# One-hot tiles of the expert gates, laid out by token

## The chip, the cores and the metric

The kernel runs on one core of a Trainium2 chip. A core has five engines that run side by side, each through a queue of its own: TensorE (PE in the profile; its weight loads are the separate row PEld), VectorE (DVE), ScalarE (ACT), GpSimd (POOL) and SyncE (SP, which here only issues DMAs). The metric is the device time of one launch in microseconds, lower being better; the number to predict is the median of the kernel after the change, against the median of the kernel before.

## The reference

Eight stages run on 256 tokens of width 1024: a retention layer, a PEER expert layer, differential attention, a second PEER layer, a gated feed-forward layer, a mixer, and a last feed-forward layer, with normalisations between them. The change touches the two PEER layers alone. Cut to what matters, one of them is:

```python
q = (xc @ w_q).reshape(tokens, 8, 2, 128)
sc = einsum('thpd,hpnd->thpn', q, subkeys)         # 8 heads, 2 halves, 128 keys each
s1, i1 = top_k(sc[:, :, 0], 16)
s2, i2 = top_k(sc[:, :, 1], 16)
top, pos = top_k(s1[..., :, None] + s2[..., None, :], 16)   # over the 256 pairs
idx = take(i1 * 128 + i2, pos)                     # 8 * 16 = 128 experts of 16384 per token
gate = softmax(top)
act = gelu(einsum('ted,td->te', u[idx], xc))
y = einsum('te,ted->td', gate * act, v[idx])
```

## The kernel before, in words

`peer` doesn't gather rows of `u` and `v`. It computes the activation of all 16384 experts for all 256 tokens and multiplies it with a gate that is zero for every expert not chosen. The activations stand in the tile `H` of 128 partitions (first key) x 128 (second key, `i2`) x 256 tokens.

A loop over the 128 values of `i2` fills `H`. Each turn takes one 512 KB block of `u` from the SP queue (`stream`, L136), splits it on ACT into a rounded half `wh` (L125) and on DVE into the rest `wl` (L126), and runs 24 matmuls of 256 columns on PE (`gemm_a`, L147 to L149). ACT then writes the gelu (L1245, or L1248 and L1250), and for the tokens whose gates are done already, DVE multiplies them in (L1251). The tiles `wh` and `wl` have three buffers each.

The router's top-k work runs on DVE beside the first turns (`route_keys`, `route`). At its end `qd` holds, by token, 128 slots with four numbers each: the first key, the second key, and the high and low part of the gate, scaled by 2^15. PE transposes the four 128 x 128 blocks of each half of the tokens (L1422) and ACT copies them into the tile `slotT`: 128 partitions (slots) x 4 numbers x 256 tokens, two bytes each (L1423).

From turn `K0` = 44 on, the 64 batches of four tokens of a layer are handled, spread over the turns up to 126. For one batch

- `onehots` has DVE compare the two index rows with the key numbers `iota4` into `o12` (L1437; the profile calls this tile `o`), and multiply the second half with the two gate parts into `og` (L1438). Both tiles come from the pool `peer_oh` with two buffers, and both have the tokens innermost: 2 x 128 keys x 4 tokens. `iota4` holds each key number four times for that.
- `gates` has PE multiply, for each token, the one-hot of the first key (weights, 128 x 128) with the two gated one-hots of the second key (256 moving columns) into `gat`, a PSUM tile with two buffers (L1448). Both operands are read with a step of four elements. ACT copies the low part out of PSUM (L1452).
- a turn later, `apply` has DVE add the high part (L1455) and multiply the gates into the finished part of `H` (L1456), and ACT copy the rest (L1458).

So a layer has 64 batches, the kernel 128, and PE runs 512 of the L1448 matmuls. The order of the instructions on each engine is set ahead of the run by a scheduler that goes by the order of the code, the raised priority of `stream` and its own estimates of times; each engine then runs its queue in order. A buffer is written again only when the last reader of its former content is done. After the loop come the 128 turns of the second product (L1276), which the change doesn't touch.

Of the kernel before, what the change touches and what calls it, by code (L numbers as in the profile page):

```python
# [12 lines left out]
F16 = mybir.dt.float16  # L13
BF16 = mybir.dt.bfloat16
U32 = mybir.dt.uint32
AF = mybir.ActivationFunctionType
ALU = mybir.AluOpType
# [3 lines left out]
T = 256  # L21
# [46 lines left out]
class Ker:  # L68
# [1096 lines left out]
    def peer(s, l, xs, units_q, units_u, units_v, ln):  # L1165
        nc, A = s.nc, s.A
        with ExitStack() as cx:
# [3 lines left out]
            H = hp.tile([128, NKEYS, T], F32, name="H")  # L1171
            cu = ExitStack()
            p = s.pool("peer_u", 1, cu)
            s.iota4 = p.tile([128, 128, 4], F16, name="iota4")
            nc.sync.dma_start(s.iota4, A["iota4"])
            with ExitStack() as ct:
                xT = s.x_transposed(p, xs, "xT", s.ln_cols(ln), s.pool("peer_t", 2, ct))
            po = s.pool("peer_oh", 2, cu)
# [23 lines left out]
            def restart():  # L1202
# [7 lines left out]
            rt = {"s16": carve([128, 2, 16, TOPK]), "i16": carve([128, 2, 16, TOPK], U32),  # L1210
                  "tmp": [carve([128, NKEYS]) for _ in range(4)]}
# [6 lines left out]
            def bank(i):  # L1218
                return (s.mm if i % 6 < 2 else s.acc)()[:, :T]

            for c in range(16):
                ps = bank(c)
# [11 lines left out]
            g = 0  # L1234
            pend = []
            for i2 in range(NKEYS):
                ps = s.mm()[:, :T]
                s.gemm_a(next(units_u), xT, ps)
                if i2 < 2:
                    if i2 == 0:  # L1240
                        scores(15)
                    s.route_keys(rt, sc, 14 + i2)
                nt = 4 * g
                if nt == 0:
                    nc.scalar.activation(H[:, i2], ps, AF.Gelu_apprx_tanh)  # L1245
                else:
                    if nt < T:
                        nc.scalar.activation(H[:, i2, nt:], ps[:, nt:], AF.Gelu_apprx_tanh)  # L1248
                    ge = p.tile([128, T], F32, name="gelu")
                    nc.scalar.activation(ge[:, :nt], ps[:, :nt], AF.Gelu_apprx_tanh)  # L1250
                    nc.vector.tensor_tensor(H[:, i2, :nt], H[:, i2, :nt], ge[:, :nt], op=ALU.mult)  # L1251
                if 2 <= i2 < K0:
                    for _ in range(ROUTE_STEPS):
                        next(route, None)
                    if i2 == K0 - 1:
                        for _ in route:
                            pass
                elif i2 >= K0:
                    for f in pend:
                        f(i2 + 1)  # L1260
                        g += 1
                    e = (i2 + 2 - K0) * (T // 4) // (NKEYS - KEND - K0)
                    pend = [s.gates(H, p, s.onehots(p, po, rt, j * 4), j) for j in range(g, min(e, T // 4))]
            assert g * 4 == T
            cu.close()
            cg.close()
# [1 line left out]
            p2 = s.pool("peer_v2", 3, cx)  # L1268
            p = s.pool("peer_v", 1, cx)
# [11 lines left out]
            for i2 in range(NKEYS):  # L1281
                v = next(units_v)
                wh = p2.tile([128, T], F32R, name="gh")
                wl = p2.tile([128, T], F32R, name="gl")
                a = nc.scalar.activation(wh, H[:, i2], AF.Copy).ins  # L1285
# [11 lines left out]
            a, b, c = last  # L1297
# [19 lines left out]
    def route(s, carve, p, rt):  # L1317

        nc = s.nc
# [6 lines left out]
        for tt in range(2):  # L1326
            a = 0
            while a < TOPK:
                n = ROWLEN[a]
                e = a  # L1330
                while e < TOPK and ROWLEN[e] == n:
                    e += 1
                o = cand[:, tt, :, ROWSTART[a]:ROWSTART[a] + n * (e - a)].rearrange("p h (a b) -> p h a b", b=n)
                sh = [128, 8, e - a, n]
                nc.vector.tensor_tensor(o, s1[:, tt, :, 0, a:e][:, :, :, None].to_broadcast(sh),
                                        s1[:, tt, :, 1, :n][:, :, None, :].to_broadcast(sh), op=ALU.add)
                a = e
# [46 lines left out]
        sh = [128, 8, TOPK, TOPK]  # L1384
# [12 lines left out]
        for tt in range(2):  # L1397
# [14 lines left out]
                                    op=ALU.is_equal)  # L1412
# [2 lines left out]
            yield  # L1415
            fold(qd[:, 1, tt].rearrange("p (h k) -> p h k", h=8))
            yield
        rt["T"] = p.tile([128, 4, T], F16, name="slotT")
        for tt in range(2):
            ps = s.paux.tile([128, 4, 128], F16, name="aux16", tag="aux")  # L1420
            for j in range(4):
                nc.tensor.transpose(ps[:, j], qd[:, j, tt], s.ident16)  # L1422
            nc.scalar.activation(rt["T"][:, :, tt * 128:tt * 128 + 128], ps, AF.Copy)  # L1423
            yield

    def onehots(s, p, p2, rt, t0):


        nc = s.nc
        sh = [128, 2, 128, 4]  # L1430

        def tok(j):
            return rt["T"][:, j:j + 2, t0:t0 + 4][:, :, None, :].to_broadcast(sh)

        o = p2.tile(sh, F16, name="o12")
        og = p2.tile(sh, F16, name="og")
        nc.vector.tensor_tensor(o, s.iota4[:, None].to_broadcast(sh), tok(0), op=ALU.is_equal)  # L1437
        nc.vector.tensor_tensor(og, o[:, 1:2].to_broadcast(sh), tok(2), op=ALU.mult)  # L1438
        return o[:, 0], og

    def gates(s, H, p, oh2, g):


        nc = s.nc
        o1, og = oh2
        ps = s.pgat.tile([128, 4, 2, 128], F32, name="gat")
        for t in range(4):
            nc.tensor.matmul(ps[:, t], o1[:, :, t], og[:, :, :, t], start=True, stop=True)  # L1448
        pv = ps.rearrange("p t a i -> p a i t")
        ts = slice(4 * g, 4 * g + 4)  # L1450
        gt = p.tile([128, NKEYS, 4], F32, name="gate")
        nc.scalar.activation(gt, pv[:, 1], AF.Copy, scale=1.0 / GSCALE)  # L1452

        def apply(k):
            nc.vector.scalar_tensor_tensor(gt, pv[:, 0], 1.0 / GSCALE, gt, op0=ALU.mult, op1=ALU.add)  # L1455
            nc.vector.tensor_tensor(H[:, :k, ts], H[:, :k, ts], gt[:, :k], op=ALU.mult)  # L1456
            if k < NKEYS:
                nc.scalar.activation(H[:, k:, ts], gt[:, k:], AF.Copy)  # L1458

        return apply  # L1460
# [23 lines left out]
def constants():  # L1484
    f32 = np.float32
    c = {}
    c["ident"] = np.eye(128, dtype=f32)
    c["ident16"] = np.eye(128, dtype=np.float16)
    pos = np.arange(T, dtype=f32)
    lin = np.linspace(0.0, 1.0, 128).astype(f32)  # L1490
    fr = (1 / (10000.0 ** lin.astype(np.float64)).astype(f32)).astype(f32)
    ang = (pos[:, None] * fr[None]).astype(f32).astype(np.float64)
    c["ret_cs"] = np.stack([np.cos(ang).astype(f32).T, np.sin(ang).astype(f32).T], 1)
    i, j = np.arange(T)[None, :], np.arange(128)[:, None]
    m = np.zeros((128, RET_HEADS, 384), f32)
    for h in range(RET_HEADS):
        lg = math.log(1.0 - 2.0 ** (-5.0 - h))
        full = np.where(i >= j, np.exp(np.maximum(i - j, 0) * lg), 0.0) * 256 ** -0.5
        m[:, h, :256] = full
        m[:, h, 256:] = full[:, :128]  # L1500
    c["ret_mask"] = m
    fr = (np.float32(500000.0) ** (-(np.arange(0, 16, 2, dtype=f32) / f32(16)))).astype(f32)
    ang = (pos[:, None] * fr[None]).astype(f32).astype(np.float64)
    dc = np.zeros((128, 3, 256), f32)
    dc[:, 0] = 1.0
    for m in (0, 64):
        for j in range(8):
            dc[m + j, 0] = dc[m + 8 + j, 0] = np.cos(ang[:, j])
            dc[m + j, 1] = -np.sin(ang[:, j])
            dc[m + 8 + j, 1] = np.sin(ang[:, j])  # L1510
            dc[m + 8 + j, 2, m + j] = 1.0
            dc[m + j, 2, m + 8 + j] = 1.0
    dc[:, 2, 128:] = np.where(np.arange(128)[None] <= np.arange(128)[:, None], 0.0, NEG)
    c["dif_cst"] = dc

    ii = np.arange(128)
    hd, tk = ii // 64, ii % 64
    same = hd[:, None] == hd[None]
    r, q = tk[:, None], tk[None]
    cm = np.zeros((128, 15, 128), f32)  # L1520
    cm[:, 0] = same / 64.0
    cm[:, 1] = cm[:, 3] = same & (r < q)
    cm[:, 2] = cm[:, 4] = same & (r <= q)
    pair1 = same & (r // 2 == q // 2)
    cm[:, 5] = pair1 & (r > q)
    cm[:, 6] = pair1 & (r < q)
    for lv in range(5):
        n = 2 << lv
        cm[:, 7 + lv] = same & (r // (2 * n) == q // (2 * n)) & (r // n > q // n)
    cm[:, 12] = dc[:, 2, 128:]  # L1530
    cm[:, 13:] = (np.arange(T) % 64 != 0).reshape(1, 2, 128)
    c["mix_cst"] = cm
    c["iota4"] = np.broadcast_to(np.arange(128, dtype=np.float16)[None, :, None], (128, 128, 4)).copy()
    cr = np.zeros((3, TOPK, TOPK), np.float16)
    for a in range(TOPK):
        cr[0, a] = ROWSTART[a]
        cr[1, a] = ROWSTART[a] - (ROWSTART[a - 1] if a else 0)
        cr[2, a] = a
    c["croute"] = np.broadcast_to(cr[None], (128, 3, TOPK, TOPK)).copy()
    return c  # L1540
# [110 lines left out]
```

## Time and profile before

| | |
|---|---|
| median of 3 runs | 2783.79 us (2776.58 to 2784.33) |
| the profiled execution | 2780.57 us |
| its span, first to last instruction | 2778.8 us |
| PE busy | 2730.4 us, 98% of the span |
| DVE busy | 2003.5 us, 72% |
| ACT busy | 1467.7 us, 53% |
| PE clock granted, mean | 0.995 of full speed |

Busy time is the time in which an engine has at least one instruction under way. Matmuls overlap each other, so the time between two starts, not the length of one, says what a matmul costs a busy PE. A time that stands behind "idle before" is the gap in front of a group of instructions, with the work that ended it.

### The profile page before, as it was taken

The page shows a single profiled execution, that of the slowest core. Times are in us where ns is not written, and L with a number is a line of the kernel's source. Part 1 is how long each engine was busy: PE and PEld are TensorE (multiplying, and loading weights), DVE is VectorE, ACT ScalarE, POOL GpSimd, SP SyncE. Part 2 cuts the span into 40 slices and gives each one's busy share as a digit, 9 for nine tenths or more (in the row PEclk, how much of TensorE's full clock was granted, in tenths as well). Part 3 has the DMA queues.
Part 4 walks back from the last instruction along what each step waited for, and adds up shares of the span by engine and source line. Part 5 has one row for each costly group of instructions (what it writes and reads, how often), then busy time and mean ns, then how long its engine had stood idle before and what let it go on. Part 6 is the DMA issues. An engine that isn't in the chain of part 4 may idle for free. (4 is left out here: it accounts for less than half of the span.)

```text
span 2778.8 us, 43988 instructions
## 1 busy us (share of the span) xinstructions
PE 2730.4 (98%) x16550; PEld 2382.0 (86%) x16550; DVE 2003.5 (72%) x3688; ACT 1467.7 (53%) x2571; POOL 7.8 (0%) x24
## 2 busy tenths in 40 slices
PE   9999999999999999999999999999999999999999
PEld 7789999998888888789999988888878887887887
DVE  7559968888666668789678887666677567665675
ACT  4445545555555555555455555555555565443654
POOL 0000000000000000000000000000000000000000
PEclk9999999999999999999999999999999999999999
DMA  6454554444556564345544445666555553221554
GB/s 212 159 178 164 185 175 149 145 145 145 194 192 196 191 196 163 99 163 177 175 157 145 145 143 183 194 193 196 191 171 190 189 167 107 69 77 61 172 186 151
DMA packets 124420, 450.69 MB, mean 162 GB/s; under 512 B 14080, under 2 KB 15120, under 8 KB 123952
## 3 DMA queue, kind: packets, MB, share of 16 engines
q1 hardware_dynamic: 124064, 447.81, 49.4%
q8 instruction: 130, 2.13, 0.3%
q14 instruction: 82, 0.67, 0.1%
q10 hardware_dynamic: 144, 0.07, 0.0%
HBM read 446.76 MB, written 1.05 MB: 161 GB/s over the span
## 5 line engine op out<-in xcount | busy, mean ns | idle before, releaser
L126 DVE TENSOR_TENSOR wl<-raw,wh 128x1024 fp32r<-128x1024 f32 x830 | 1014.6, 1223 | 436.3 <-ACT wh L125 435.2
L125 ACT ACTIVATE wh<-raw 128x1024 fp32r<-128x1024 f32 x830 | 879.3, 1060 | 731.9 <-PE mm L148 387.5
L147 PE MATMUL mm<-xT,wh 128*128 128x256 f32 x2384 | 696.4, 293 | 6.7 <-ACT gelu L1250 3.6
L149 PE MATMUL mm<-xT,wl 128*128 128x256 f32 x2384 | 678.1, 285 | 1.8 <-DVE wl L126 1.8
L148 PE MATMUL mm<-xT,wh 128*128 128x256 f32 x2384 | 678.5, 285 | 0.0
L147 PEld LDWEIGHTS mm<-xT,wh 128*128 128x128 f32 x2384 | 456.7, 192 | 23.2 <-ACT gelu L1250 7.1
L148 PEld LDWEIGHTS mm<-xT,wh 128*128 128x128 f32 x2384 | 457.4, 192 | 3.4 <-DVE xT L261 0.3
L149 PEld LDWEIGHTS mm<-xT,wl 128*128 128x128 f32 x2384 | 455.7, 191 | 4.2 <-DVE wl L126 2.4
L1276 PE MATMUL acc<-wl,gh 128*128 128x512 f32 x1024 | 317.4, 389 | 0.3
L1276 PE MATMUL acc<-wh,gl 128*128 128x512 f32 x1024 | 316.6, 389 | 0.0
L1276 PE MATMUL acc<-wh,gh 128*128 128x512 f32 x1024 | 277.8, 389 | 3.2 <-ACT gh L1285 3.2
L1285 ACT ACTIVATE gh<-H 128x256 fp32r<-128x256 f32 x256 | 106.5, 418 | 298.6 <-PE acc L1276 298.6
L1276 PEld LDWEIGHTS acc<-wh,gh 128*128 128x128 f32 x1024 | 192.0, 188 | 43.5 <-ACT gh L1285 3.6
L1276 PEld LDWEIGHTS acc<-wl,gh 128*128 128x128 f32 x1024 | 192.2, 188 | 41.0 <-DVE wl L126 1.1
L1276 PEld LDWEIGHTS acc<-wh,gl 128*128 128x128 f32 x1024 | 192.2, 188 | 39.9
L1286 DVE TENSOR_TENSOR gl<-H,gh 128x256 fp32r<-128x256 f32 x256 | 108.4, 425 | 115.9 <-PE acc L1276 115.9
L159 PE MATMUL mm<-xT,wh 128*128 128x512 f32 x406 | 146.2, 397 | 0.8 <-ACT wh L125 0.6
L1448 PE MATMUL gat<-og,o 128*128 128x256 f16 x512 | 137.7, 407 | 2.7 <-DVE gate L1455 2.7
L1437 DVE TENSOR_TENSOR o<-iota,slotT 128x1024 f16<-128x1024 f16 x128 | 88.3, 691 | 65.2 <-PE gat L1448 64.8
L160 PE MATMUL mm<-xT,wl 128*128 128x256 f32 x406 | 113.9, 280 | 0.8 <-DVE wl L126 0.8
L159 PE MATMUL aux<-xT,wh 128*128 128x512 f32 x294 | 105.0, 393 | 0.0
L182 PE MATMUL acc<-wl,xT 128*128 128x512 f32 x256 | 104.1, 407 | 0.0
(538 smaller groups left out, 3893.3 us busy)
## 6 DMA issues: line engine op xcount, KB each, us to landing
raw<-peer_u SPq DMA_DIRECT2D x256, 512.0 KB, 3.7
raw<-peer_v SPq DMA_DIRECT2D x256, 512.0 KB, 4.4
raw<-ffn_w SPq DMA_DIRECT2D x132, 512.0 KB, 4.5
raw<-peer_q SPq DMA_DIRECT2D x32, 512.0 KB, 3.7
raw<-ret_qk SPq DMA_DIRECT2D x16, 512.0 KB, 4.1
raw<-ret_v SPq DMA_DIRECT2D x16, 512.0 KB, 4.0
raw<-ret_g SPq DMA_DIRECT2D x16, 512.0 KB, 3.8
raw<-ret_o SPq DMA_DIRECT2D x16, 512.0 KB, 4.2
```

Source lines behind the costliest of these rows:

```text
L125: a = nc.scalar.activation(h, ap, AF.Copy)
L126: d = nc.vector.tensor_tensor(l, ap, h.bitcast(F32), op=ALU.subtract)
L147: nc.tensor.matmul(out, w[0][:, c], x[0][:, d], start=start and d == 0, stop=False)
L148: nc.tensor.matmul(out, w[0][:, c], x[1][:, d], start=False, stop=False)
L149: nc.tensor.matmul(out, w[1][:, c], x[0][:, d], start=False, stop=stop and d == ND - 1)
L159: nc.tensor.matmul(ps, w[0][:, c], x, start=d == 0, stop=False)
L160: nc.tensor.matmul(ps[:, :T], w[1][:, c], both[:, d, 0], start=False, stop=False)
L182: nc.tensor.matmul(outs[tt], x[0][:, d, t], w[1][:, c], start=False, stop=False)
L1276: mm = nc.tensor.matmul(accs[cb][tt], a[:, t], b[:, cb * 512:cb * 512 + 512], start=i2 == 0 and wi == 0, stop=i2 == NKEYS - 1 and wi == 2)
L1285: a = nc.scalar.activation(wh, H[:, i2], AF.Copy).ins
L1286: d = nc.vector.tensor_tensor(wl, H[:, i2], wh.bitcast(F32), op=ALU.subtract).ins
L1448: nc.tensor.matmul(ps[:, t], o1[:, :, t], og[:, :, :, t], start=True, stop=True)
```

## The change

The one-hot tiles get the order token, part, key, with the keys side by side, so that the matmuls read both operands without a step. Two consecutive keys then share the same index, and to give DVE a run of two elements with a step of one on that operand too, the slot numbers are stored twice: `slotI` and `slotG` have 256 tokens x 2 numbers x 2 copies each. ACT fills them with two copies for each half of the tokens, in place of one. `iota` holds each key number once. `og` moves from the pool with two buffers to the pool `peer_u` with one. The number and the sizes of the DVE operations and of the matmuls stay.

```diff
-            s.iota4 = p.tile([128, 128, 4], F16, name="iota4")
-            nc.sync.dma_start(s.iota4, A["iota4"])
+            s.iota = p.tile([128, 128], F16, name="iota")
+            nc.sync.dma_start(s.iota, A["iota"])
...
-                    pend = [s.gates(H, p, s.onehots(p, po, rt, j * 4), j) for j in range(g, min(e, T // 4))]
+                    pend = [s.gates(H, p, s.onehots(p, po, rt, j), j) for j in range(g, min(e, T // 4))]
...
-        rt["T"] = p.tile([128, 4, T], F16, name="slotT")
+        for n in "IG":
+            rt[n] = p.tile([128, T, 2, 2], F16, name="slot" + n)
...
-            nc.scalar.activation(rt["T"][:, :, tt * 128:tt * 128 + 128], ps, AF.Copy)
+            for j, n in enumerate("IG"):
+                nc.scalar.activation(rt[n][:, tt * 128:tt * 128 + 128],
+                                     ps[:, 2 * j:2 * j + 2].rearrange("p a t -> p t a")[:, :, :, None].to_broadcast(
+                                         [128, 128, 2, 2]), AF.Copy)
...
-        sh = [128, 2, 128, 4]
-
-        def tok(j):
-            return rt["T"][:, j:j + 2, t0:t0 + 4][:, :, None, :].to_broadcast(sh)
-
-        o = p2.tile(sh, F16, name="o12")
-        og = p2.tile(sh, F16, name="og")
-        nc.vector.tensor_tensor(o, s.iota4[:, None].to_broadcast(sh), tok(0), op=ALU.is_equal)
-        nc.vector.tensor_tensor(og, o[:, 1:2].to_broadcast(sh), tok(2), op=ALU.mult)
-        return o[:, 0], og
+        sh = [128, 8, 64, 2]
+        t4 = slice(4 * g, 4 * g + 4)
+        tok = lambda t: t[:, t4].rearrange("p t a e -> p (t a) e")[:, :, None, :].to_broadcast(sh)
+        v = lambda t: t.rearrange("p t a (k e) -> p (t a) k e", e=2)
+        o = p2.tile([128, 4, 2, 128], F16, name="o12")
+        og = p.tile([128, 4, 2, 128], F16, name="og")
+        io = s.iota.rearrange("p (k e) -> p k e", e=2)[:, None].to_broadcast(sh)
+        nc.vector.tensor_tensor(v(o), io, tok(rt["I"]), op=ALU.is_equal)
+        nc.vector.tensor_tensor(v(og), o[:, :, 1:2].to_broadcast([128, 4, 2, 128]), tok(rt["G"]), op=ALU.mult)
+        return o[:, :, 0], og
...
-            nc.tensor.matmul(ps[:, t], o1[:, :, t], og[:, :, :, t], start=True, stop=True)
+            nc.tensor.matmul(ps[:, t], o1[:, t], og[:, t], start=True, stop=True)
```

## Rows read from the trace of the kernel before

**Rows 1.** The page, busy time of each engine.
```profile
PE 2730.4 (98%) x16550; PEld 2382.0 (86%) x16550; DVE 2003.5 (72%) x3688; ACT 1467.7 (53%) x2571; POOL 7.8 (0%) x24
```
**Rows 2.** Groups of instructions by line: busy us, mean ns, idle before.
```profile
L1448 PE MATMUL gat<-og,o 128*128 128x256 f16 x512 | 137.7, 407 | 2.7 <-DVE gate L1455 2.7
L1437 DVE TENSOR_TENSOR o<-iota,slotT 128x1024 f16<-128x1024 f16 x128 | 88.3, 691 | 65.2 <-PE gat L1448 64.8
L1438 DVE TENSOR_TENSOR og<-o,slotT 128x1024 f16<-128x1024 f16 x128 | 87.5, 684 | 0.0
```
**Rows 3.** Timeline of PE around one batch: start us, length us, instruction.
```profile
501.73 0.28 PE L149 MATMUL mm<-xT,wl 128*128 128x256 f32 x1
501.86 1.09 PE L1448 MATMUL gat<-og,o 128*128 128x256 f16 x4
502.58 0.48 PE L147 MATMUL mm<-xT,wh 128*128 128x256 f32 x1
502.90 0.28 PE L148 MATMUL mm<-xT,wh 128*128 128x256 f32 x1
```
**Rows 4.** Timeline of PE, a run of matmuls on zeros.
```profile
2584.79 2.35 PE L270 MATMUL mm<-zeros 128*128 128x256 bf16 x20
```
**Rows 5.** Instructions of lines L270 and L1448: ns min/median/max, first and last start.
```profile
L270 PE MATMUL mm<-zeros x172: 272/273/421, 1.1 to 2586.9; 128*128 128x256 bf16 x172
L270 PEld LDWEIGHTS <-zeros x172: 96/98/151, 1.1 to 2586.8; 128*128 128x128 bf16 x172
L1448 PEld LDWEIGHTS <-o x512: 112/117/139, 351.6 to 1684.3; 128*128 128x128 f16 x171
```
**Rows 6.** PE, three transposes of the router: timeline, then the group of L1422.
```profile
1364.38 0.34 PE L1422 MATMUL aux<-H 128*128 128x128 f16 x3
...
L1422 PE MATMUL aux<-H 128*128 128x128 f16 x16 | 2.3, 224 | 0.0
```
**Rows 7.** Busy time in stretches: length, busy us (count) by engine, clock, DMA.
```profile
300.00:345.00 45.00, 45.00 (x377) 44.79 (x377) 42.19 (x101) 24.06 (x36) 0.00 (x0) 1.00 0.58 187
405.00:560.00 155.00, 154.43 (x1170) 142.28 (x1169) 128.41 (x214) 87.73 (x194) 0.00 (x0) 1.00 0.45 149
560.00:703.00 143.00, 140.42 (x1058) 128.11 (x1057) 125.73 (x196) 76.35 (x177) 0.00 (x0) 1.00 0.44 144
1395.00:1540.00 145.00, 145.00 (x1099) 133.62 (x1098) 120.01 (x201) 83.12 (x185) 0.00 (x0) 1.00 0.46 150
1540.00:1692.00 152.00, 147.54 (x1108) 134.26 (x1105) 133.50 (x209) 81.29 (x190) 0.00 (x0) 1.00 0.44 143
```
**Rows 8.** The same stretches, PE instructions of L1448 alone.
```profile
405.00:560.00 155.00, 34.64 (x128) 1.00 0.45 149
560.00:703.00 143.00, 31.13 (x116) 1.00 0.44 144
1395.00:1540.00 145.00, 32.81 (x122) 1.00 0.46 150
1540.00:1692.00 152.00, 32.95 (x124) 1.00 0.44 143
```
**Rows 9.** Groups of DVE instructions in the router, by line.
```profile
L1401 DVE TENSOR_TENSOR H<-H 128x2048 f16<-128x2048 f16 x4 | 9.2, 2288 | 0.1
...
L1405 DVE TENSOR_TENSOR H<-H 128x2048 f16<-128x2048 f16 x4 | 4.9, 1219 | 0.0
```
**Rows 10.** Timelines of DVE and PE around one batch.
```profile
472.77 0.69 DVE L1438 TENSOR_TENSOR og<-o,slotT 128x1024 f16<-128x1024 f16 x1
...
473.25 1.09 PE L1448 MATMUL gat<-og,o 128*128 128x256 f16 x4
```
**Rows 11.** Timeline of ACT, first slot copy and second gate copy.
```profile
344.01 0.59 ACT L1423 ACTIVATE slotT<-aux 128x512 f16<-128x512 f16 x1
...
410.45 0.58 ACT L1452 ACTIVATE gate<-gat 128x512 f32<-128x512 f32 x1
```
**Rows 12.** Waits over the whole span: us in total, times, longest.
```profile
DVE o L1437 <- PE gat L1448: 64.8, 96, 1.4
```
**Rows 13.** DMA issues: count, KB each, us to landing.
```profile
iota<-iota SPq DMA_DIRECT2D x2, 128.0 KB, 4.2
```

More of the change, by code (lines that the diff above doesn't have):

```diff
@@ L1422, in route, with onehots @@
                 nc.tensor.transpose(ps[:, j], qd[:, j, tt], s.ident16)
-            nc.scalar.activation(rt["T"][:, :, tt * 128:tt * 128 + 128], ps, AF.Copy)
+            for j, n in enumerate("IG"):
+                nc.scalar.activation(rt[n][:, tt * 128:tt * 128 + 128],
+                                     ps[:, 2 * j:2 * j + 2].rearrange("p a t -> p t a")[:, :, :, None].to_broadcast(
+                                         [128, 128, 2, 2]), AF.Copy)
             yield
-    def onehots(s, p, p2, rt, t0):
+    def onehots(s, p, p2, rt, g):
         nc = s.nc
-        sh = [128, 2, 128, 4]
-        def tok(j):
-            return rt["T"][:, j:j + 2, t0:t0 + 4][:, :, None, :].to_broadcast(sh)
-        o = p2.tile(sh, F16, name="o12")
-        og = p2.tile(sh, F16, name="og")
-        nc.vector.tensor_tensor(o, s.iota4[:, None].to_broadcast(sh), tok(0), op=ALU.is_equal)
-        nc.vector.tensor_tensor(og, o[:, 1:2].to_broadcast(sh), tok(2), op=ALU.mult)
-        return o[:, 0], og
+        sh = [128, 8, 64, 2]
[8 more added lines that the diff above has]
+        return o[:, :, 0], og
     def gates(s, H, p, oh2, g):
@@ L1532, in constants @@
     c["mix_cst"] = cm
-    c["iota4"] = np.broadcast_to(np.arange(128, dtype=np.float16)[None, :, None], (128, 128, 4)).copy()
+    c["iota"] = np.broadcast_to(np.arange(128, dtype=np.float16), (128, 128)).copy()
     cr = np.zeros((3, TOPK, TOPK), np.float16)
```

## Prediction

> **What bounds the kernel now.** I read the page's busy times first: PE is busy for 98% of the span, DVE for 72%, ACT for 53% [rows 1]. So time is won where PE gets less to do, or lost where another engine makes it wait. Busy time alone doesn't say that PE works at its best rate, so the second view is the timeline of PE around one batch of gates. The matmuls of the loop start every 0.12 us. The four of L1448 take 1.09 us from the first start to the last end at a mean length of 0.407 us, so they start every (1.09 - 0.407) / 3 = 0.228 us; and from the L149 in front of them to the second matmul behind them it is 502.90 - 501.73 = 1.17 us, where two starts alone would need 0.24: 0.93 us for a batch [rows 2, 3]. The reader is to see that a matmul of 256 columns costs PE twice as much here as one line away.
>
> The third view is busy time by stretch, over the two stretches in which the batches run, each cut in half. There DVE is no bystander: it is busy for 128.4 of 155, 125.7 of 143, 120.0 of 145 and 133.5 of 152 us, which is 83, 88, 83 and 88% [rows 7]. The later half is fuller since the multiplications into `H` grow with the turns. PE already misses 2.6 and 4.5 us in the two later halves, and under 1 us in the earlier ones. What the change gives PE therefore has to get past DVE.
>
> **PE, the saving.** The matmuls keep their number and size; what changes is that 256 moving columns and 128 weights lie side by side in place of eight bytes apart. The nearest row without a step is the run of 20 matmuls on zeros, also 256 columns of two bytes and 128 weights, each with its own weight load: (2.35 - 0.273) / 19 = 0.109 us from start to start [rows 4, 5]. The weight loads with the step are only a little longer, 117 against 98 ns [rows 5]. That loading a new block of two-byte weights each time need not slow the matmul shows in three transposes of different blocks, 128 columns each: (0.34 - 0.224) / 2 = 0.058 us apart [rows 6]. So I take 0.109 us: 4 x (0.228 - 0.109) = 0.474 us less for a batch, and 128 x 0.474 = 60.6 us if PE never waits. The other end is no saving, should the step not be the cause.
>
> [...]
>
> **DVE, the one-hots.** The two operations keep their size, 1024 elements at 0.69 us [rows 2]. In the router, 2048 elements of two bytes take 1.22 us where both operands run on with a step of one (L1405) and 2.29 us where one operand repeats a single element along the innermost axis (L1401) [rows 9]; 0.69 us lies on the fast side of that. Before, the shortest run was four tokens; after, it is the two stored copies. No row has a run of two. Bounds: 0, and half of 2.29 - 1.22, that is 0.53 us, for each of two operations. I take 0, as the run still has a step of one, as L1405 has and L1401 has not.
>
> **ACT, the slot copies.** Four copies of 512 elements become eight, each with a step in PSUM. The nearest row with such a step, the gate copy, takes 0.58 us against 0.59 us for the old copy [rows 11], so this is 4 x 0.6 = 2.4 us more on ACT in all, and no less than 0. It lies ahead of what waits for it: the first copy stands at 344.01 us, the first gate copy that the loop's pace asks for at 410.45 us [rows 11]. Without that cover it would be 2.4 us. The load of `iota` shrinks from 128 to 32 KB, twice, in the SP queue ahead of the layer [rows 13]: 0, at most the 4.2 us to its landing once a layer.
>
> **The wait that is added.** `og` has one buffer now. At 472.77 us DVE writes an `og`, and at 473.25 us, before that is done, PE starts the four matmuls of an earlier one [rows 10]: DVE works a batch ahead, and that is no longer allowed. It will wait for the matmuls in front of `og` as it now waits in front of `o`, 64.8 us over 96 times [rows 12]. Behind it in DVE's queue stand `wl` and the multiplications into `H`, for which PE and ACT wait. Bounds: below, 0, since a batch is followed by most of a turn of 24 x 0.12 = 2.9 us of other matmuls in which `og` (0.69 us) fits; above, all of `og` exposed each time, 128 x 0.69 = 88 us. I take it as part of the next term.
>
> **What DVE lets through.** How busy can DVE be before PE stalls? In the stretch from 300 to 345 us it is busy for 42.19 of 45 us, 93.8%, and PE misses nothing; in the last stretch PE misses time at 88% [rows 7]. I take 93.8%, and 88% as the other end. Each half then takes the longer of its length less 0.474 us for each batch, and its DVE time over 0.938. The batches are the L1448 instructions over four: 32, 29, 30.5 and 31 [rows 8].
>
> - 405 to 560: 155 - 15.2 = 139.8 against 136.9; saved 15.2.
> - 560 to 703: 143 - 13.7 = 129.3 against 134.0; saved 9.0.
> - 1395 to 1540: 145 - 14.5 = 130.5 against 127.9; saved 14.5.
> - 1540 to 1692: 152 - 14.7 = 137.3 against 142.3; saved 9.7.
>
> That is 48.4 us, and the 5.5 batches that lie ahead of these stretches add 2.6: 51 us. The two earlier halves come up to the density at which the later ones now lose 2.6 and 4.5 us, so I take off 7 us for such stalls, the wait for `og` among them: 44 us. The profiled execution took 2780.6 us; 2780.6 - 44 = 2736.6. The median of the runs shown is 3.2 us above that execution, within their own spread, and I round to 2738 us. At 88% the same four lines give 152 - 128.4/0.88 and so on: 9.1, 0.1, 8.6 and 0.3, with the 2.6 some 21 us, or 2760 us; with PE alone in the way it is 2720 us.
>
> **Rivals.**
>
> - *DVE takes most of it.* The 88% case, 2755 to 2772 us. For it: the stalls in the later halves; against it: the stretch at 93.8% without one. 20%.
> - *The step is not the cause, and nothing is won.* 0.228 us stays; 2780 to 2786 us, the time of before. For it: nothing in the trace changes the step alone; against it: same columns, same element size, half the time. 7%. [...]
> - *Slower: the single `og`.* The loop runs `og`, matmuls, `og` in turn, and PE stands while `og` is made. It decides when more than 44 / 128 = 0.34 us of the 0.69 is exposed in each batch; with all of it, 2737 + 88 = 2825 us. Against it: the 2.9 us of other matmuls between two batches. 4%.
> - *Slower: the runs of two fall to the slow rate.* 1.06 us more for a batch, 128 x 1.06 = 136 us on DVE. For the first layer that is 254 + 61 x 1.06 = 319 us in a stretch of 298; over 0.938 it is 340, so 42 us more, and about 2865 us for both layers; 2825 us if DVE were never idle. 5%. [...]
>
> **How the numbers follow.** My forecast, PE's saving cut down by DVE in the later halves, has 62% and its own range of 2720 to 2755 us, which ends at the PE-only sum; 2% are left for more than that. A measurement of this kernel tells about 0.3%, some 8 us, from no change. Faster by more than that: the forecast, the first rival and the rest, 62 + 20 + 2, and 1 of the others, 85%. Within it: 6%. Slower: 9%. The range to hold 8 in 10 is the forecast's and the nearer three quarters of the first rival's: 2718 to 2767 us.
>
> **What would show it.** The L1448 matmuls start every 0.11 us and a batch costs PE about 0.46 us in place of 0.93; their weight loads fall to about 98 ns; L1437 and L1438 stay at 0.69 us (1.2 us would show the slow rate); DVE's share in the two stretches rises to 90% or more, most in the later halves, with waits of DVE on L1448 now in front of L1438 too; the time outside the two stretches stays. Wrong would be: L1448 still at 0.23 us, PE waiting for L1438, or a scheduler that orders other stages anew and moves time there.

## The result, and the profile after

The changed kernel takes 2749.51 us (median of 4 runs, 2747.9 to 2751.4) against 2784.06 us before (now the median of 4 runs): 34.6 us less, a ratio of 0.988 with a 95% interval of 0.9859 to 0.9901. The forecast was 2738 us, in a range of 2718 to 2767 us. The profiled execution took 2750.62 us; its span is 30.0 us shorter than the 2778.8 us before.

The page, busy time of each engine of the kernel after:

```profile
span 2748.8 us, 44032 instructions
...
PE 2674.3 (97%) x16550; PEld 2360.8 (86%) x16550; DVE 2004.6 (73%) x3688; ACT 1472.8 (54%) x2575; POOL 7.8 (0%) x24
```

PE is busy for 56.1 us less than in [rows 1], and the span is 30.0 us shorter. So PE's idle time, span less busy, rose from 48.4 (2778.8 - 2730.4) to 74.5 us, by 26.1. DVE's work is the same to about a microsecond. The 30.0 us are these two numbers: what PE was given, less what it lost again to waits.

The groups of instructions by line (busy us, mean ns, idle before and its releaser), the answer to [rows 2]; the lines of `onehots` and `gates` have moved by four to six:

```profile
L1453 PE MATMUL gat<-og,o 128*128 128x256 f16 x512 | 78.3, 275 | 3.1 <-DVE og L1443 3.1
L147 PE MATMUL mm<-xT,wh 128*128 128x256 f32 x2384 | 685.9, 288 | 29.8 <-ACT gelu L1250 26.6 <-ACT ge L259 2.3 <-DVE rope_b L429 0.5
...
L1443 DVE TENSOR_TENSOR og<-o,slotG 128x1024 f16<-128x1024 f16 x128 | 88.1, 688 | 29.8 <-PE gat L1453 28.8
L1442 DVE TENSOR_TENSOR o<-iota,slotI 128x1024 f16<-128x1024 f16 x128 | 87.4, 684 | 0.0
```

The one-hot operations stay at 0.69 us, with runs of two. The wait for PE's matmuls now stands in front of `og` and no longer in front of `o`. The timeline of PE around one batch, and the instructions of L1453 (ns min/median/max), the answer to [rows 3, 5]:

```profile
501.16 0.28 PE L148 MATMUL mm<-xT,wh 128*128 128x256 f32 x1
501.28 0.61 PE L1453 MATMUL gat<-og,o 128*128 128x256 f16 x4
501.65 0.36 PE L149 MATMUL mm<-xT,wl 128*128 128x256 f32 x1
501.85 0.28 PE L147 MATMUL mm<-xT,wh 128*128 128x256 f32 x1
```

```profile
L1453 PEld LDWEIGHTS <-o x512: 95/98/99, 352.4 to 1655.9; 128*128 128x128 f16 x171
L1453 PE MATMUL gat<-og,o x512: 272/273/283, 352.4 to 1656.0; 128*128 128x256 f16 x171
```

The four matmuls start every (0.61 - 0.273) / 3 = 0.112 us, and from the L148 in front to the second matmul behind it is 0.69 us, 0.45 more than two starts of 0.12: a batch costs PE 0.45 us where it was 0.93. Busy time by stretch (length, then PE, PEld, DVE, ACT, POOL, clock, DMA), over the two stretches with batches in two parts each, the answer to [rows 7]:

```profile
405.00:540.00 135.00, 130.89 (x1093) 127.55 (x1092) 117.96 (x197) 82.70 (x179) 0.00 (x0) 1.00 0.48 159
540.00:690.00 150.00, 136.94 (x1131) 131.65 (x1129) 137.78 (x214) 83.74 (x193) 0.00 (x0) 1.00 0.46 151
1380.00:1515.00 135.00, 130.89 (x1092) 127.56 (x1091) 118.02 (x197) 83.37 (x181) 0.00 (x0) 1.00 0.48 159
1515.00:1664.00 149.00, 136.27 (x1125) 130.98 (x1123) 137.07 (x213) 83.08 (x190) 0.00 (x0) 1.00 0.46 150
```

PE is idle for 4.1, 13.1, 4.1 and 12.7 us there, 34.0 in all, where the stretches of [rows 7] had 7.6. That is the 26 us. DVE is at 87 and 92%: in the earlier parts PE now waits although DVE is a good way from full. Of the waits of the whole span (us in total, times, longest), these belong to the batches and to the turns around them:

```profile
PEld mm L147 <- ACT gelu L1250: 33.4, 24, 1.7
ACT gate L1457 <- DVE H L1461: 30.9, 41, 2.1
DVE og L1443 <- PE gat L1453: 28.8, 62, 0.9
PE mm L147 <- ACT gelu L1250: 26.6, 24, 1.4
ACT H L1463 <- DVE gate L1460: 25.0, 22, 1.8
ACT gelu L1250 <- DVE H L1251: 16.0, 24, 1.6
```

PE hardly waits for the one-hots: 3.1 us in front of L1453. It waits 26.6 us, in 24 places, for a PSUM bank `mm` that ACT has yet to read with its gelu (the row of PEld has its weight loads waiting in the same 24 places). One of these places, on ACT and then on PE:

```profile
609.62 1.06 ACT L125 ACTIVATE wh<-raw 128x1024 fp32r<-128x1024 f32 x1 [0.87 <-PE mm L148]
610.58 0.21 ACT L1248 ACTIVATE H<-mm 128x68 f32<-128x68 f32 x1
610.69 0.32 ACT L1250 ACTIVATE gelu<-mm 128x184 f32<-128x184 f32 x1
...
611.06 0.38 PE L147 MATMUL mm<-xT,wh 128*128 128x256 f32 x1 [0.91 <-ACT gelu L1250]
```

The gelu stands in ACT's queue behind the split `wh` of a further block, and that split has to wait until PE's L148 is done with the buffer. So ACT is idle for 0.87 us, the gelu is late, and PE waits 0.91 us for it. In 22 of the 24 places ACT's last idle time before the gelu is this one, in front of `wh`; in the other two it is in front of the gate copy, for DVE. So ACT's waits for DVE in the list above (30.9, 25.0 and 16.0 us) are not what ends last in front of PE, but for these two places.

### The profile page after: what moved, and what is told of

It reads as the page before. It is cut to its first block, busy times and chain, and to the rows that moved or that the text cites. A ratio compares the mean times of both kernels' runs of the same rounds, so it can differ in the third digit from the quotient of the medians.

```text
span 2748.8 us, 44032 instructions
## 1 busy us (share of the span) xinstructions
PE 2674.3 (97%) x16550; PEld 2360.8 (86%) x16550; DVE 2004.6 (73%) x3688; ACT 1472.8 (54%) x2575; POOL 7.8 (0%) x24
## 5 line engine op out<-in xcount | busy, mean ns | idle before, releaser
L147 PE MATMUL mm<-xT,wh 128*128 128x256 f32 x2384 | 685.9, 288 | 29.8 <-ACT gelu L1250 26.6
L148 PE MATMUL mm<-xT,wh 128*128 128x256 f32 x2384 | 677.7, 284 | 0.0
L147 PEld LDWEIGHTS mm<-xT,wh 128*128 128x128 f32 x2384 | 457.3, 192 | 39.7 <-ACT gelu L1250 33.4
L148 PEld LDWEIGHTS mm<-xT,wh 128*128 128x128 f32 x2384 | 458.2, 192 | 0.8 <-DVE xT L261 0.3
L1443 DVE TENSOR_TENSOR og<-o,slotG 128x1024 f16<-128x1024 f16 x128 | 88.1, 688 | 29.8 <-PE gat L1453 28.8
L183 PE MATMUL acc<-wh,xT 128*128 128x512 f32 x256 | 101.8, 400 | 0.0
```

What stands on the lines that cost most here:

```text
L147: nc.tensor.matmul(out, w[0][:, c], x[0][:, d], start=start and d == 0, stop=False)
L148: nc.tensor.matmul(out, w[0][:, c], x[1][:, d], start=False, stop=False)
L183: mm = nc.tensor.matmul(outs[tt], x[1][:, d, t], w[0][:, c], start=False, stop=stop and j == 1)
```

## The experiments

Two questions were open: whether the step was really PE's cost, and what took back 26 us. Code that is left out of an edit is marked by `...`. All are edits of the kernel after unless another is named.

**Which step costs.** Four runs read other columns or keys of the same tiles, so that the size of the matmuls stays and a step differs.

```diff
+        mv = og.rearrange("p t a i -> p (t a i)").rearrange("p (k s) -> p s k", s=4)
...
-            nc.tensor.matmul(ps[:, t], o1[:, t], og[:, t], start=True, stop=True)
+            nc.tensor.matmul(ps[:, t], o1[:, t], mv[:, t], start=True, stop=True)
```

> The kernel after, but the 256 moving columns of each gate matmul are read from the same tile with a step of four elements (so the columns are the wrong ones); the weights stay without a step. If the step of the moving columns was the cost: a start every 0.22 to 0.23 us in place of 0.11, a batch 0.9 us, and 2775 to 2790 us. If it was the step of the weights: 0.11 us and 2745 to 2755 us. If two steps together were needed: in between, or as the second.

```diff
+        wt = o1.rearrange("p t a i -> p (t a i)")[:, :512].rearrange("p (k s) -> p s k", s=4)
...
-            nc.tensor.matmul(ps[:, t], o1[:, t], og[:, t], start=True, stop=True)
+            nc.tensor.matmul(ps[:, t], wt[:, t], og[:, t], start=True, stop=True)
```

Here `onehots` returns the whole tile `o`.

> The kernel after, but the 128 weights of each gate matmul are read with a step of four elements (the wrong keys); the moving columns stay without a step. If the moving step was the cost: weight loads of 112 to 117 ns as before, a start every 0.11 to 0.12 us, 2745 to 2755 us. [...]

```diff
+        mv = og.rearrange("p t a i -> p (t a i)").rearrange("p (h k s) -> p h s k", h=2, s=2)
...
-            nc.tensor.matmul(ps[:, t], o1[:, t], og[:, t], start=True, stop=True)
+            nc.tensor.matmul(ps[:, t], o1[:, t], mv[:, t // 2, t % 2], start=True, stop=True)
```

> As the run with a moving step of four, with a step of two (wrong columns). If what counts is the bytes that a column spans, four bytes as in the 32-bit matmuls of the loop that start every 0.12 us: 0.11 us, the time of the kernel after. If any step breaks the fast read: 0.22 us or more.

```diff
+        mv = og.rearrange("p t a i -> p (t a i)").rearrange("p (k s) -> p s k", s=8)
...
-            nc.tensor.matmul(ps[:, t], o1[:, t], og[:, t], start=True, stop=True)
+            nc.tensor.matmul(ps[:, t], o1[:, t], mv[:, 2 * t:2 * t + 2], start=True, stop=True)
```

> As the run with a moving step of four, with a step of eight (two runs of 128 columns, wrong ones). If the cost goes with the bytes spanned: twice that of a step of four, a start every 0.43 us, and some 50 us more than before. If a step costs the same whatever its size: 0.22 to 0.23 us and the time of before.

Measured: moving step of four, 2795.57 us (ratio to before 1.0048, interval 1.0031 to 1.0065); weights' step of four, 2751.5 us (0.9889, 0.987 to 0.9908); moving step of two, 2752.69 us and of eight, 2902.63 us in one run each. For each kernel, one batch in PE's timeline and the instructions of its line (ns min/median/max); first the moving step of four:

```profile
502.11 1.07 PE L1454 MATMUL gat<-og,o 128*128 128x256 f16 x4
```

```profile
L1454 PE MATMUL gat<-og,o x512: 387/405/408, 351.8 to 1704.0; 128*128 128x256 f16 x171
```

the moving step of two:

```profile
500.56 0.63 PE L1454 MATMUL gat<-og,o 128*128 128x256 f16 x4
```

```profile
L1454 PE MATMUL gat<-og,o x512: 274/276/288, 351.4 to 1658.1; 128*128 128x256 f16 x171
```

the moving step of eight:

```profile
503.27 1.97 PE L1454 MATMUL gat<-og,o 128*128 128x256 f16 x4
```

```profile
L1454 PE MATMUL gat<-og,o x512: 609/629/632, 350.1 to 1805.9; 128*128 128x256 f16 x171
```

and the weights' step of four:

```profile
501.06 0.63 PE L1454 MATMUL gat<-og,o 128*128 128x256 f16 x4
```

```profile
L1454 PEld LDWEIGHTS <-o x512: 110/114/133, 352.0 to 1656.6; 128*128 128x128 f16 x171
L1454 PE MATMUL gat<-og,o x512: 272/273/302, 352.0 to 1656.7; 128*128 128x256 f16 x171
```

From start to start, (first number less the median length) / 3: 0.118 us with a step of two, 0.222 with four, 0.447 with eight, against 0.112 without one. So for these two-byte columns 4 bytes from one to the next cost about what 2 do, 8 bytes twice and 16 four times as much. The weights' step lengthens their load from 98 to 114 ns and makes little of the difference: (0.63 - 0.273) / 3 = 0.119 us from start to start, and 2751.5 against 2749.51 us. The step of the moving columns alone brings back 0.222 of the 0.228 us, so it was nearly the whole of it.

The run with a step of four has another message: with PE's work as before the change, it is 14 us slower than before (2781.12 us beside it). Something else in the change costs time.

**What that is: the single buffer.** First its part alone, in the kernel before:

```diff
-        og = p2.tile(sh, F16, name="og")
+        og = p.tile(sh, F16, name="og")
```

> The kernel before with og in the pool with one buffer, all else as it was. If the single buffer costs time by itself, about as much as it did when the step of four was put back into the kernel after (2795.6 against 2781 us): 10 to 20 us more than before, 2793 to 2803 us. If it only bites when DVE is as full as in the kernel after: within 5 us of before.

Measured 2800.06 us, 18.7 us more than before (2781.38 us beside it); ratio 1.006 (1.0043 to 1.0077). Its waits over the span:

```profile
DVE og L1438 <- PE gat L1448: 63.9, 88, 1.3
ACT gate L1452 <- DVE H L1456: 36.2, 39, 2.5
ACT H L1458 <- DVE gate L1455: 30.2, 24, 2.2
PE mm L147 <- ACT gelu L1250: 16.0, 24, 0.9
```

and from the kernel before the same wait of ACT and, of those that waited for the gelu L1250 (us, times), PE:

```profile
ACT H L1458 <- DVE gate L1455: 8.4, 6, 2.2
...
  PE mm L147: 3.6, 6
```

DVE waits for the gate matmuls no longer in all than in [rows 12], 63.9 against 64.8 us. But the copy into `H` waits for DVE 30.2 us in place of 8.4, and PE for the gelu 16.0 us in place of 3.6, in 24 places in place of 6.

Then the buffer given back, in the kernel after. To make room for it, `gate` is kept in 16 bits, and a run with that alone is the control:

```diff
-        gt = p.tile([128, NKEYS, 4], F32, name="gate")
+        gt = p.tile([128, NKEYS, 4], F16, name="gate")
```

> The kernel after with the tile gate in 16 bits in its one buffer and og in its one buffer: what the run with two og buffers has, without the second buffer (the gates are rounded to 16 bits). If the second buffer of og was what won 20 us there: within 3 us of the kernel after, 2747 to 2754 us. If the 16 bits won them: 2728 to 2735 us.

```diff
-        og = p.tile([128, 4, 2, 128], F16, name="og")
+        og = p2.tile([128, 4, 2, 128], F16, name="og")
...
-        gt = p.tile([128, NKEYS, 4], F32, name="gate")
+        gt = p.tile([128, NKEYS, 4], F16, name="gate")
```

> The kernel after with two buffers for og, as before the change; to make room, gate is kept in 16 bits in its one buffer (the gates are rounded to that). If the added wait for og matters: the 29 us of DVE in front of og go and the time falls by some 5 to 15 us, to 2735 to 2745 us. If it only stands where DVE would be idle: within 3 us of the kernel after.

Measured: 16 bits alone 2746.51 us (0.9877, 0.986 to 0.9894), like the kernel after; with the second `og` 2729.47 us (0.9814, 0.9797 to 0.9831). The second buffer is worth 17 us, by the ratios 0.6%. A wait and the busy time by stretch of the latter:

```profile
PE mm L147 <- ACT gelu L1250: 11.8, 20, 1.4
405.00:540.00 135.00, 134.53 (x1130) 131.88 (x1129) 121.84 (x205) 85.22 (x187) 0.00 (x0) 1.00 0.51 166
540.00:675.00 135.00, 128.72 (x1061) 123.70 (x1060) 126.59 (x199) 76.95 (x179) 0.00 (x0) 1.00 0.46 152
```

In the earlier part DVE now reaches 90% and PE loses 0.5 us in place of 4.1; in the later one DVE stands at 93.8% and PE loses 6.3.

**The other single buffers.** A rival was that `og` has little to do with it, and that it is `gelu` and `gate`, which ACT and DVE pass to each other.

```diff
-                    ge = p.tile([128, T], F32, name="gelu")
+                    ge = po.tile([128, T], F32, name="gelu")
```

> The kernel after with two buffers for the tile gelu in place of one. If DVE's load is what PE waits for: no more than 4 us less, 2745 to 2750 us. If PE waits since ACT's gelu waits for the single buffer (16 us over 24 times in the kernel after): 2730 to 2740 us.

```diff
-                    ge = p.tile([128, T], F32, name="gelu")
+                    ge = po.tile([128, T], F32, name="gelu")
...
-                    pend = [s.gates(H, p, s.onehots(p, po, rt, j), j) for j in range(g, min(e, T // 4))]
+                    pend = [s.gates(H, po, s.onehots(p, po, rt, j), j) for j in range(g, min(e, T // 4))]
...
-        gt = p.tile([128, NKEYS, 4], F32, name="gate")
+        gt = p.tile([128, NKEYS, 4], F16, name="gate")
```

> The kernel after with two buffers for both tiles that ACT and DVE pass to each other, gelu and gate; to make room, gate is kept in 16 bits (the gates are rounded to that). DVE's operations keep their number and sizes. If DVE's load is what PE waits for: within 5 us of the kernel after. If the single buffers make ACT wait in its queue (31 us in front of the gate copy, 16 us in front of the gelu), and PE behind it: 2720 to 2735 us.

Measured: `gelu` alone 2753.64 us (0.9893, 0.9877 to 0.991), nothing; both 2730.57 us (0.9812, 0.9796 to 0.9829), 19 us less than the kernel after, with DVE's operations as many and as long. With 16 bits alone and two `gelu` alone winning nothing, this is put down to the second `gate`, which was not tried by itself: it wins about what a second `og` does. The waits of that run, where those of the gate copy and of the copy into `H` for DVE had been 30.9 and 25.0 us:

```profile
ACT gate L1457 <- PE gat L1453: 25.2, 28, 2.3
DVE og L1443 <- PE gat L1453: 18.5, 44, 1.0
PE mm L147 <- ACT gelu L1250: 12.5, 10, 1.6
ACT H L1463 <- DVE gate L1460: 6.0, 12, 1.7
```

The pure form of the DVE theory, that only its load counts, falls here: the load stayed, and PE's idle time, span less busy, is 2728.1 - 2674.3 = 53.8 us in place of 74.5. PE waits for the gelu in 10 places in place of 24.

**DVE's load.** The second one-hot operation left out, and with it the gates; PE reads the plain one-hots:

```diff
-        og = p.tile([128, 4, 2, 128], F16, name="og")
...
-        nc.vector.tensor_tensor(v(og), o[:, :, 1:2].to_broadcast([128, 4, 2, 128]), tok(rt["G"]), op=ALU.mult)
-        return o[:, :, 0], og
+        return o[:, :, 0], o
```

> The kernel after without the second one-hot operation: the gate parts aren't multiplied in, and PE reads the plain one-hots as moving columns (the gates are left out). DVE has 128 x 0.6 = 77 us less to do, PE the same. If DVE's load holds PE back: PE's idle time falls back from 74 to some 48 us and the time to 2718 to 2728 us. If it is the order and the single buffers of the tiles between ACT and DVE, whatever DVE's load: 2735 to 2750 us.

Measured 2708.38 us (0.9732, 0.9715 to 0.9749), 10 us below what either theory gave. Busy time by stretch:

```profile
405.00:540.00 135.00, 135.00 (x1136) 132.60 (x1135) 106.67 (x179) 84.69 (x190) 0.00 (x0) 1.00 0.51 165
540.00:670.00 130.00, 129.02 (x1084) 126.49 (x1082) 111.66 (x171) 78.83 (x183) 0.00 (x0) 1.00 0.50 164
```

DVE is at 79 and 86%, and PE loses 1.0 us. 2720 us had been the time of before less 60.6 us; but before has 7.6 us of stalls in these stretches of its own, and they go as well. The run also takes the single `og` away, so it doesn't part load from buffer. Two of its waits:

```profile
ACT gate L1455 <- DVE H L1459: 33.6, 36, 1.5
ACT H L1461 <- DVE gate L1458: 31.1, 34, 1.2
```

ACT waits for DVE here as long as in the kernel after, where it was 30.9 and 25.0 us, and yet PE never waits for the gelu. So it is not these waits that hold PE back.

**One copy of the slot numbers.**

```diff
-            rt[n] = p.tile([128, T, 2, 2], F16, name="slot" + n)
+            rt[n] = p.tile([128, T, 2], F16, name="slot" + n)
...
-        sh = [128, 8, 64, 2]
+        sh = [128, 8, 128]
...
-        tok = lambda t: t[:, t4].rearrange("p t a e -> p (t a) e")[:, :, None, :].to_broadcast(sh)
+        tok = lambda t: t[:, t4].rearrange("p t a -> p (t a)")[:, :, None].to_broadcast(sh)
```

with ACT's copy, `v` and `io` to match.

> The kernel after with each slot number stored once, so that one operand of both one-hot operations repeats a single element along the innermost axis. By the router's two rows, 2.29 against 1.22 us for 2048 elements: 1.22 us for each of the two operations in place of 0.69, 136 us more for DVE, which is then the bound: 2820 to 2870 us. If the repeated element costs nothing here: 2747 to 2754 us.

Measured 2896.66 us (1.0414, 1.0397 to 1.0432), 147 us more than the kernel after and above the range expected. The groups by line:

```profile
L1442 DVE TENSOR_TENSOR og<-o,slotG 128x1024 f16<-128x1024 f16 x128 | 156.1, 1219 | 42.3 <-PE gat L1452 42.2
L1441 DVE TENSOR_TENSOR o<-iota,slotI 128x1024 f16<-128x1024 f16 x128 | 155.5, 1216 | 0.0
```

The durations came out as the router's rows gave them [rows 9]: 0.69 us and half of the 1.07 between the two rows, 1.22 us. The stalls around them were underestimated. The stored copies carry the whole change: without them it loses 115 us.

**A version that beats both.** PE adds the two gate parts in PSUM, so that `gate`, ACT's copy and DVE's addition go, and the room goes to a second `og`:

```diff
-        ps = s.pgat.tile([128, 4, 2, 128], F32, name="gat")
+        ps = s.pgat.tile([128, 4, 128], F32, name="gat")
         for t in range(4):
-            nc.tensor.matmul(ps[:, t], o1[:, t], og[:, t], start=True, stop=True)
+            for j in range(2):
+                nc.tensor.matmul(ps[:, t], o1[:, t], og[:, t, j], start=j == 0, stop=j == 1)
...
+            nc.vector.scalar_tensor_tensor(H[:, :k, ts], pv[:, :k], 1.0 / GSCALE, H[:, :k, ts], op0=ALU.mult, op1=ALU.mult)
             if k < NKEYS:
-                nc.scalar.activation(H[:, k:, ts], gt[:, k:], AF.Copy)
+                nc.scalar.activation(H[:, k:, ts], pv[:, k:], AF.Copy, scale=1.0 / GSCALE)
```

`gat` gets four buffers, and `pv` is the tile with tokens and keys swapped.

> A version that might beat both: the high and the low part of the gate are added by PE in PSUM (eight matmuls of 128 columns for a batch in place of four of 256), so the tile gate, ACT's copy into it and DVE's addition go (some 77 us on each), og has its two buffers back and gat four. If DVE was what held PE back, PE is alone in the way: 2705 to 2715 us, as without the og operation (2708 us). [...]

Measured 2720.53 us (0.9773, 0.9756 to 0.9791), 29 us below the kernel after and 61 below before, though 5 to 15 above what was expected. Busy time by stretch:

```profile
405.00:540.00 135.00, 135.00 (x1234) 133.29 (x1232) 104.19 (x172) 67.13 (x155) 0.00 (x0) 1.00 0.52 164
540.00:672.00 132.00, 132.00 (x1216) 130.36 (x1215) 111.77 (x170) 62.37 (x152) 0.00 (x0) 1.00 0.50 161
```

PE is never idle here, so it is alone in the way. PE's busy time is 2679.1 us against 2666.7 in the run without `og`: eight matmuls of 128 columns for a batch, in the places that this kernel's order gives them, cost 12.4 us more than four of 256, over 128 batches 0.10 us each. The run changes several things at once, so it doesn't tell what each of them wins.

**A rival that no run isolates: the order of ACT's queue.** The order is set ahead of the run, and the traces show that it isn't the same in these kernels. Each layer has 82 turns with an L1250, 164 in all. In most of them the splits `wh` in ACT's queue are a fixed number of blocks ahead of the gelu's turn; in some they are one block further, as in the place shown under the result, and the gelu stands behind one more split. The turns of the second kind, counted from ACT's order in each trace, and PE's waits for the gelu (L147, PE's own row):

| kernel | turns with one more `wh` ahead of the gelu | waits of PE | us |
|---|---|---|---|
| before | 20 | 6 | 3.6 |
| before, one `og` | 28 | 24 | 16.0 |
| after, and with 16 bits alone | 28 | 24 | 26.6 |
| after, two `gelu` | 26 | 26 | 28.8 |
| after, two `og` | 20 | 20 | 11.8 |
| after, two `gelu` and two `gate` | 10 | 10 | 12.5 |
| without the second one-hot operation | 0 | 0 | 0 |
| gates added in PSUM | 0 | 0 | 0 |
| one copy of the slot numbers | 69 | 68 | 125.0 |

Every wait of PE for the gelu stands at such a turn, but for one of the 68 in the last row. The kernels with one `og`, one `gelu` and one `gate` share one order of their gelus and splits, whatever the step of the moving columns; before and the kernel after with two `og` share another. Between the kernels after with two `og` and with one, PE's waits at these turns differ by 26.6 - 11.8 = 14.8 us, most of the 17. This points to the order that the scheduler makes of a single buffer, but it is read from the traces and not shown by a run: why the scheduler moves the turns, and what a single `og` would cost in an unchanged order, stays open.

## Why the prediction was right, and what was mis-sized

- *PE's saving, 60.6 us.* Right, with 56.1 us less of PE's busy time: 0.112 us from start to start against the 0.109 taken, a batch 0.45 us against 0.46, and the cause is the moving step, now shown apart from the weights' step; a step of two, which reads other columns too, stays near the rate without a step (0.118 us).
- *DVE's one-hots at 0.* Right: 0.684 and 0.688 us. The row for its failure was right too, 1.22 us, but its price of 2865 us was 32 short of the 2896.66 measured.
- *ACT's copies and the load of `iota` at 0.* No wait for them stands among the longest; they were not tried alone.
- *What DVE lets through, at 93.8%: 51 us.* The number came out near, partly by luck. The run with two `og`, which has all of the change but the single buffer, is 54.3 us below the kernel before that was measured beside it (2783.81 - 2729.47), and DVE stands at 93.8% in its later part. But the trace shows no limit of DVE there: 5.4 of the 6.3 us that PE loses in that part are waits for the gelu, which are all at turns with one more split ahead of it. The 93.8% had been read in a stretch ahead of the first batch (351.6 us), of other work. In the kernel after the two earlier parts, for which the forecast had PE alone in the way, lost 4.1 us each with DVE at 87%. That only DVE's load sets the loss is refuted by the run with two `gate` buffers; what a lighter DVE is worth by itself stays open, since the run without the second one-hot operation has another order too.
- *The wait that is added, "as part of the next term": 7 us for it and for stalls together.* This is the term that was mis-sized. The single `og` costs 18.7 us in the kernel before and 17 us in the kernel after. With 17 in place of 7, the sum is 2780.6 - 51 + 17 = 2746.6 us, against 2750.62 in the profiled execution. In all the forecast had waits take back 60.6 - 44 = 16.6 us, and they took 26.1. The lower bound of 0 was argued from PE's side: 2.9 us of other matmuls, in which 0.69 us fits. PE indeed hardly waits for `og`. The prediction then looked behind `og` in DVE's queue; what the traces show is ACT's queue, in which 28 gelus in place of 20 stand behind one more split. A scheduler that orders other work anew was on the prediction's list of what would be wrong, without a price.
- *The rivals.* That DVE takes most (2755 to 2772 us) was 5 us off at its near end; the step as no cause, and the slow rate, are out. The slower end of the single `og` did not come: it would have had to cost 0.34 us a batch beyond the forecast, and costs 17 / 128 = 0.13 in all.

Left open: whether two buffers for `og` and for `gate` together win more than either, which was not tried; and how much of the price of a single buffer is the order of the queues and how much the wait itself, as no run holds the order fixed.

## What to carry to other kernels

Look at the start-to-start time of a matmul, not at its busy share: PE was 98% busy while its gate matmuls ran at half the rate of the kernel after (0.228 us from start to start against 0.112), and what halved it was that the moving operand was read eight bytes apart (0.222 us with that step alone), not the weights (0.119). When work is taken from the bounding engine, ask which buffers between the others become single by the same edit, and compare the order of each engine's queue in the two traces: the price of the single buffer, a third of the gain, did not show in DVE's total wait, but in which work ACT had in front of the gelu. If an operand must be repeated along the innermost axis, storing it twice to keep runs of two was enough here for DVE's faster rate on two-byte elements: 0.69 us for 1024 of them, where one stored copy took 1.22.

## What the runs showed of the hardware that was not expected

The two-byte moving columns of the gate matmuls ran at nearly the rate without a step when they stood four bytes apart (0.118 us for 256 columns at a step of two, 0.112 without a step), at half of it at eight bytes (0.222), at a quarter at sixteen (0.447). A step of four in their weights cost 16 ns more in the load (114 against 98) and 0.007 us more from start to start (0.119). Two copies of an element were as good for DVE's one-hot operations as a run of four (0.684 and 0.688 us against 0.691 and 0.684), and one repeated element was not (1.22).
